# Blocks turned by VectorE and moved by way of DRAM instead of TensorE transposes, in a hybrid decoder layer

## The chip, the cores and the metric

The kernel runs on one core of a Trainium2 chip. The metric is the device time of one execution in microseconds, median of three runs. TensorE multiplies matrices, VectorE (DVE in the profile) and ScalarE (ACT) work on tiles, GpSimd (POOL) and SyncE (SP) issue DMAs. The profile is one more execution, taken by the hardware profiler.

## The reference

One decoder layer for 256 tokens and 2048 features, in float32. The input is normalised and projected; the projections feed two parallel mixers, whose outputs are merged under gates and projected once more.

```python
h = _rmsnorm(x, pre_norm_g)
proj = jnp.einsum('bsd,de->bse', h, w_in)
(q_a, c_kv, k_rope, z_mla, c_in, b_gate, c_gate, z_conv, g_mla, g_conv) = jnp.split(proj, cuts, axis=-1)
# latent attention, 16 heads: q from q_a, k_nope and v from c_kv, rotary parts, causal softmax p
attn = p @ v                                          # per head, 256 x 128
attn = attn.reshape(b, s, MLA_WIDTH) * jax.nn.silu(z_mla)
y_mla = jnp.einsum('bse,ed->bsd', attn, w_o_mla)
u = c_gate * c_in                                     # short convolution of 3 taps
conv = sum(conv_w[k] * u_pad[:, k:k + s] for k in range(CONV_K))
y_conv = jnp.einsum('bse,ed->bsd', b_gate * conv * jax.nn.silu(z_conv), w_o_conv)
merged = jax.nn.sigmoid(g_mla) * y_mla + jax.nn.sigmoid(g_conv) * y_conv
out = jnp.einsum('bsd,de->bse', merged, w_out)
x = x + _rmsnorm(out, post_norm_g)
```

## The kernel before

**Precision and weights.** Every float32 operand is split into a high and a low part (`split_act`: ScalarE writes the high part, VectorE subtracts for the low one), and a product is three matmuls: high by high, high by low, low by high. The weights come in units of 128 x 2048 elements in the order of the list `plan`. `take(i)` loads ahead into three raw buffers and splits one unit ahead, in halves of 1024 columns, into five pairs of buffers `whi` and `wlo`. SyncE issues the loads. TensorE's instructions, and operations marked by `keep_in_program_order`, keep the order of the program; the other operations of ScalarE and VectorE are placed by a scheduler when the program is built. On the chip each engine then runs its instructions in that fixed order.

**Stages.** First the two latents are projected and normalised (to about 60 us). Then a loop over 16 heads (60 to 600 us). A head `h` projects its gate (`project`, tile z), makes its scores and softmax (`scores`, tiles sc and p; p holds three 128 x 128 blocks: queries of the first tile by keys of the first, queries of the second by both), turns p so that keys lie on partitions (`turn`, tiles tp and pt) and multiplies by the values (`values`, tile o). In between the same head makes a quarter of the channels of the convolution branch: `channels(h, 0)` to `channels(h, 3)`, 24 products of weights with the normalised input each (tile cv, weights u_head). Four heads complete one block of 512 channels, in two token tiles, which `taps` moves along the tokens by DMA (tiles mv, cw, issued by POOL) and `channels_join` multiplies by the last factor. Every second head makes queries and keys for the next pair (`group_a`, tiles qn and kn), every fourth the values (`group_v`).

Then come four column blocks c (600 to 955 us). Each has four products over 2048 features, `tokens(c, n, ...)`: two gates from the input (n = 0, 1), the attention (n = 2), the channels (n = 3). `split_branch` splits the attention's outputs into at_both during the first, `turn_branch` turns the channel blocks into cv_both during n = 1 and 2 of c = 0. The merged block m of c is turned by `features` during the first product of c + 1, into m_both. Last the output product: four column blocks of four units each, the first one begun before the last merged block is turned.

All turning is done by TensorE: `transpose` into a PSUM bank, whose content is then split. `turn` makes three transposes of 128 x 128 a head, `turned` four for each of eight channel blocks and eight merged blocks. The product of probabilities and values begins with a matmul that reads both parts of pt:

```python
mm(both, vv[0][:, 0, vs], pt[:, :, :S], start=True, stop=False)
```

Many temporaries come from one pool, `bp`; when the heads are done it is closed, and at_both and cv_both lie in its memory.

Of the kernel before, what the change touches and what calls it, by code (L numbers as in the profile page):

```python
# [11 lines left out]
F32 = mybir.dt.float32  # L12
# [6 lines left out]
P = 128  # L19
S = 256  # L20
NT = S // P
D = 2048
KD = D // P
H = 16
# [58 lines left out]
def tile_layer(ctx: ExitStack, tc: tile.TileContext, xw, x, pos, pvec, post_g, wc, wz, wcv, wkr, wqk, wqr, wv, cwr, wsq, out):  # L83
    nc = tc.nc
# [15 lines left out]
    wpool = ctx.enter_context(tc.tile_pool(name="wpool", bufs=1))  # L100
    psum = ctx.enter_context(tc.tile_pool(name="psum", bufs=1, space=PSUM))


    plan = []

    def add(ap, width=UNIT):
        plan.append((ap, width))
        return len(plan) - 1
# [24 lines left out]
            u_head[i][j] = add(wcv[i, j - 1] if j else wz[i])  # L133

    u_d = [[[add(wsq[n, c, k]) for k in range(4)] for n in range(4)] for c in range(4)]
    u_out = [[add(wsq[4, c, k]) for k in range(4)] for c in range(4)]

    raws, splits, early = {}, {}, {}
    done = {"raw": 0, "split": 0}
# [13 lines left out]
    def split_unit(i):  # L153
        t, w = raws.pop(i), plan[i][1]
        parts = []
        if i == u_kr:
            t = t[:, :w].rearrange("p (k c) -> p k c", k=KD)
            for h in range(2):
                both = wpool.tile([P, HALF], F32R, name=f"whi{i}_{h}", tag="whi", bufs=5)
                both = both[:, :].rearrange("p (k j c) -> p k j c", k=KD // 2, j=2)  # L160
                ks = slice(h * KD // 2, (h + 1) * KD // 2)
                split_act(both[:, :, 0], both[:, :, 1], t[:, ks])
                parts.append(both.rearrange("p k j c -> p k (j c)"))
            splits[i] = parts
            return
        if i <= u_qa[-1]:

            hi, lo = (wpool.tile([P, HALF], F32R, name=f"{o}{i}", tag=o, bufs=5) for o in ("whi", "wlo"))
            for j in range(2):
                k, o = 2 * i + j, j * XW  # L170
                src = x_first if k == 0 else t[:, o : o + S]
                split_scaled(x_both, src, k)
                split_act(hi[:, j * R : (j + 1) * R], lo[:, j * R : (j + 1) * R], t[:, o + S : o + XW], True)
            splits[i] = [(hi, lo)]
            return
        for h in range(0, w, HALF):
            n = min(HALF, w - h)
            if u_out[3][0] <= i < u_out[3][3]:
                hi, lo = (op.tile([P, HALF], F32R, name=f"w{o}{i}_{h}") for o in ("hi", "lo"))
            else:  # L180
                hi = wpool.tile([P, HALF], F32R, name=f"whi{i}_{h}", tag="whi", bufs=5)
                lo = wpool.tile([P, HALF], F32R, name=f"wlo{i}_{h}", tag="wlo", bufs=5)
            split_act(hi[:, :n], lo[:, :n], t[:, h : h + n])
            parts.append((hi, lo))
        splits[i] = parts
# [23 lines left out]
    def bank(name, tag="mm", bufs=4):  # L209
        return psum.tile([P, 512], F32, name=name, tag=tag, bufs=bufs)  # L210
# [80 lines left out]
    def temp(name, shape=(P, S), dt=F32, bufs=2, tag=None):  # L291

        tag, n = tag or name.rstrip("0123456789_"), shape[-1]
        if n % LINE == 0:
            return bp.tile(list(shape), dt, name=name, tag=tag, bufs=bufs)
        return bp.tile([P, -(-n // LINE) * LINE], dt, name=name, tag=tag, bufs=bufs)[:, :n]


    def split_scaled(dst, src, k):
# [251 lines left out]
    def scores(h):  # L551
# [35 lines left out]
        for t in range(NT):  # L587
            o = slice(t * P, (2 * t + 1) * P)
            nc.vector.tensor_scalar(p[:, o], p[:, o], rs[:, t : t + 1], None, op0=ALU.mult)
        return p  # L590

    def turn(h, p):

        tp = bank(f"tp{h}", tag="st", bufs=1)
        for b in range(3):
            transpose(tp[:, b * P : (b + 1) * P], p[:, b * P : (b + 1) * P], ident[:, :])
        pt = temp("pt", (P, 2, 3 * P), F32R, 1)
        split_act(pt[:, 0, :], pt[:, 1, :], tp[:, : 3 * P])
        return pt

    def values(h, pt, sz):
# [52 lines left out]
    def channels_join(j, t):  # L654
        u, w = cv_t[:, j, t, :], cv_w[:, t, :]
        nc.vector.tensor_tensor(u, u, w, op=ALU.mult)

    def taps(j, t):

# [35 lines left out]
    for h in range(H):  # L695

        tapped = h % 4 == 2 or (h > 0 and h % 4 == 0) or h == H - 1
        sz_new = silu("sz", project(u_head[h][0], f"z{h}"))
        if h == 0:
            latent_turn("qa", qa, "q_g", (("st", 1), ("o", 1)))  # L700

            def turn_keys():
                latent_turn("ckv", ckv, "kv_g", (("mm", 4), ("mm", 4)))
                next(table_parts)

            channels(h, 0, turn_keys)
            for i in first:
                make(*i)
            key_rope()
            channels(h, 1)  # L710
            channels(h, 2)
            p = scores(h)
        elif h == 1:

            pt = turn(0, p)
            channels(h, 0)
            values(0, pt, sz)
            p = scores(h)
            channels(h, 1)
            channels(h, 2)  # L720
            pt = turn(h, p)
        else:
            p = scores(h)
            channels(h, 0)
            channels(h, 1)
            pt = turn(h, p)
            if tapped:
                next(tap)
            channels(h, 2)
            values(h, pt, sz_new)  # L730
            if tapped:
                next(tap)
        for i in made[h]:
            make(*i)
        if h == 1:
            values(h, pt, sz_new)
        sz = sz_new
        channels(h, 3)
        if h % 4 == 0 and h > 0:
            for t in range(NT):  # L740
                channels_join(h // 4 - 1, t)
        if h % 4 == 1:
            tap = taps(h // 4, 1)
            next(tap)
        elif h % 4 == 3 and h + 1 < H or h == H - 2:
            tap = taps(h // 4, 0)
            next(tap)
    for t in range(NT):
        channels_join(3, t)


    bstack.close()
# [8 lines left out]
            hs = slice(h, h + 2)  # L761
            split_act(at_both[:, hs, :S], at_both[:, hs, S:], at_f[:, hs, :], True)

    def turn_branch(i):

        j, t = divmod(i, NT)
        turned(f"ct{i}", cv_t[:, j, t, :], cv_both, j, t)

    def turned(name, src, both, c, t):
        tp = bank(name, tag=("st", "o")[t], bufs=1)  # L770
        for j in range(4):
            transpose(tp[:, j * P : (j + 1) * P], src[:, j * P : (j + 1) * P], ident[:, :])
        ks, ts = slice(4 * c, 4 * c + 4), slice(t * P, (t + 1) * P)
        lo = slice(t * P + S, (t + 1) * P + S)
        split_act(both[:, ks, ts], both[:, ks, lo], tp[:, :].rearrange("p (k q) -> p k q", k=4))

    def tokens(c, n, cols):

        pss = [bank(f"sq{c}_{n}_{t}") for t in range(NT)]
        for kk in range(4):  # L780
            w = take(u_d[c][n][kk])
            if c == 0 and n == 0:
                split_branch(kk)
            if c == 0 and n in (1, 2):
                turn_branch(4 * (n - 1) + kk)
            for t in range(NT):
                for k4 in range(4):
                    k = 4 * kk + k4
                    a = [cols[:, k, o + t * P : o + (t + 1) * P] for o in (0, S)]
                    product(pss[t][:, :], a, w(k4, 512), k == 0, k == KD - 1)  # L790
        return pss
# [4 lines left out]
    def features(c, m, m_both):  # L796

        for t in range(NT):
            turned(f"mt{c}_{t}", m[t], m_both, c, t)

    waiting = m_both = None
    for c in range(4):
# [18 lines left out]
        for t in range(NT):  # L821
            nc.vector.tensor_tensor(m[t][:, :], pss[t][:, :], m[t][:, :], op=ALU.mult)
        pss = tokens(c, 3, cv_both)
        for t in range(NT):
            y = gates[1][t]
            nc.vector.tensor_tensor(y[:, :], pss[t][:, :], y[:, :], op=ALU.mult)
            nc.vector.tensor_tensor(m[t][:, :], m[t][:, :], y[:, :], op=ALU.add)
        waiting = m
    def out_product(ps, t, w, kk):
        ts = slice(t * P, (t + 1) * P)  # L830
# [5 lines left out]
        for t in range(NT):  # L836
            out_product(pss[t], t, w, kk)

    pss = [bank(f"out0_{t}") for t in range(NT)]
    out_products(pss, take(u_out[0][0]), 0)  # L840
    features(3, waiting, m_both)
    main.close()


# [27 lines left out]
    def finish(t, rr):  # L872
        for a, b in ((0, 256), (256, 512), (512, 1024), (1024, 1536), (1536, 2048)):
# [3 lines left out]
            )  # L877
            nc.sync.dma_start(out=out[t * P : (t + 1) * P, cs], in_=og[:, t, cs])

    for c in range(3):  # L880
        if c:
            pss = [bank(f"out{c}_{t}") for t in range(NT)]
        for kk in range(0 if c else 1, 4):
            out_products(pss, take(u_out[c][kk]), kk)
        for t in range(NT):
            out_block(c, t, pss[t])
    nc.vector.reduce_sum(part[:, :], ssq[:, :, :3], axis=mybir.AxisListType.X)
    nc.vector.tensor_scalar(part[:, :], part[:, :], 1.0 / D, EPS, op0=ALU.mult, op1=ALU.add)
    pss = [bank(f"out3_{t}") for t in range(NT)]
    for t in range(NT):  # L890
        for kk in range(4):
            if t == 0:
                last.append(take(u_out[3][kk]))
            out_product(pss[t], t, last[kk], kk)
        finish(t, out_block(3, t, pss[t]))

# [89 lines left out]
```

## Time and profile before

| | |
|---|---|
| median of 3 runs | 1053.41 us (1053.41 to 1053.55) |
| the profiled execution | 1052.91 us, span 1050.9 us, granted TensorE clock 0.998 |
| DMA | 212.13 MB, mean 202 GB/s |
| heads, 100 to 350 us | TensorE busy 250.00, VectorE 181.59, ScalarE 151.10, POOL 14.43 us |
| column blocks, 665 to 960 us | TensorE busy 295.00, VectorE 150.02, ScalarE 123.65, POOL 0.00 us |

The span runs from the first to the last instruction; the execution's own time is some 2 us longer. The page gives the busy time of each engine, the chain of work that ended last (each step followed back to what released it), groups of instructions by source line, and DMA issues. Other views of the same trace list an engine's instructions in order of time (start, length, line, tile written <- tiles read, and in brackets its idle time before and what ended it), the waits by engine, and the time from a DMA's issue to its landing. PE is TensorE, PEld its weight loads. Line L88 is the helper `matmul`, L91 `transpose`, L228 and L229 the two halves of `split_act`, L664 the helper that issues the taps' DMAs.

### The profile page before, as it was taken

How to read it: one execution, taken by the hardware profiler on the slowest of the kernel's cores; microseconds unless marked ns; L12 is line 12 of the kernel's file. 1: busy time of each engine (PE TensorE's matmuls, PEld its weight loads, DVE VectorE, ACT ScalarE, POOL GpSimd, SP SyncE). 2: the span in 40 equal slices, each digit the busy share in tenths (PEclk: the TensorE clock that was granted, in tenths of full speed). 3: DMA queues.
4: the chain of work that ended last, by engine and by line, in shares of the span. 5: the costliest groups of instructions: out<-in, count | busy, mean ns of one | idle time of the engine just before them, and what ended most of it. 6: DMA issues, size and time to landing. Idle time of an engine off the chain costs nothing.

```text
span 1050.9 us, 12889 instructions
## 1 busy us (share of the span) xinstructions
PE 1041.9 (99%) x4934; PEld 874.3 (83%) x4934; DVE 670.0 (64%) x954; ACT 560.3 (53%) x770; POOL 71.4 (7%) x147
## 2 busy tenths in 40 slices
PE   9999999999999999999999999999999999999996
PEld 8888888888888888888888888888888888888885
DVE  7588668676686777866777764554554455445562
ACT  7776556556665566655655464444434434444450
POOL 7620011000110001100011000000000000000000
PEclk9999999999999999999999999999999999999999
DMA  8745566455665555845567555455555555558542
GB/s 332 298 173 200 201 219 207 165 210 200 210 215 196 189 192 175 273 172 193 188 203 236 202 184 196 166 195 200 190 187 184 200 200 190 176 195 314 196 171 80
DMA packets 33884, 212.13 MB, mean 202 GB/s; under 512 B 4320, under 2 KB 5024, under 8 KB 10912
## 3 DMA queue, kind: packets, MB, share of 16 engines
q1 hardware_dynamic: 29808, 197.54, 52.1%
q0 software_dynamic: 3584, 10.50, 4.2%
q10 hardware_dynamic: 432, 3.29, 0.8%
q8 instruction: 38, 0.62, 0.2%
q14 instruction: 22, 0.18, 0.0%
HBM read 205.05 MB, written 2.10 MB: 197 GB/s over the span
## 4 chain that ended last, share of the span: by engine, by line
PE 98%; issue 1%; DVE 0%; POOL 0%; ACT 0%; POOLq 0%; DVEq 0%; ACTq 0%
PE cv L88 33%; PE sq L88 33%; PE z L88 8%; PE out L88 7%; PE qn L88 2%; PE kn L88 2%; PE qa L88 2%; PE vv L88 2%; PE ckv L88 2%; PE sc L88 1%; PE qr L88 1%; PE o L88 1%; PE tp L91 0%; PE idle L88 0%; PE kr L88 0%
## 5 line engine op out<-in xcount | busy, mean ns | idle before, releaser
L229 DVE TENSOR_TENSOR wlo<-raw,whi 128x1024 fp32r<-128x1024 f32 (+1 forms) x370 | 440.3, 1199 | 309.4 <-ACT whi L228 285.5
L228 ACT ACTIVATE whi<-raw 128x1024 fp32r<-128x1024 f32 (+1 forms) x372 | 383.5, 1036 | 379.2 <-PE sq L88 186.3
L88 PE MATMUL cv<-whi,x_both 128*128 128x512 f32 x1024 | 325.4, 391 | 0.0
L88 PEld LDWEIGHTS cv<-whi,x_both 128*128 128x128 f32 x1024 | 192.3, 188 | 38.9
L88 PE MATMUL cv<-wlo,x_both 128*128 128x512 f32 x512 | 199.5, 390 | 0.0
L88 PE MATMUL sq<-whi,x_both 128*128 128x512 f32 x512 | 160.2, 391 | 0.0
L88 PEld LDWEIGHTS sq<-whi,x_both 128*128 128x128 f32 x512 | 96.1, 188 | 19.9
L88 PEld LDWEIGHTS cv<-wlo,x_both 128*128 128x128 f32 x512 | 96.2, 188 | 18.5
L88 PE MATMUL sq<-wlo,x_both 128*128 128x512 f32 x256 | 99.6, 389 | 0.0
L88 PE MATMUL sq<-whi,at_both 128*128 128x512 f32 x256 | 80.4, 391 | 0.0
L88 PE MATMUL sq<-whi,cv_both 128*128 128x512 f32 x256 | 79.5, 389 | 0.0
L88 PE MATMUL out<-whi,m_both 128*128 128x512 f32 x256 | 79.2, 390 | 0.0
L88 PE MATMUL z<-x_both,whi 128*128 128x512 f32 x256 | 60.7, 389 | 0.0
L88 PEld LDWEIGHTS sq<-whi,cv_both 128*128 128x128 f32 x256 | 48.0, 188 | 10.0
L88 PEld LDWEIGHTS sq<-whi,at_both 128*128 128x128 f32 x256 | 48.1, 188 | 9.9
L88 PEld LDWEIGHTS out<-whi,m_both 128*128 128x128 f32 x256 | 48.0, 188 | 9.9
L88 PEld LDWEIGHTS z<-x_both,whi 128*128 128x128 f32 x256 | 48.0, 188 | 9.9
L88 PEld LDWEIGHTS sq<-wlo,x_both 128*128 128x128 f32 x256 | 48.1, 188 | 9.8
L88 PE MATMUL sq<-wlo,at_both 128*128 128x512 f32 x128 | 49.8, 389 | 0.0
L88 PE MATMUL sq<-wlo,cv_both 128*128 128x512 f32 x128 | 49.8, 389 | 0.0
L88 PE MATMUL out<-wlo,m_both 128*128 128x512 f32 x128 | 49.8, 389 | 0.0
L88 PEld LDWEIGHTS z<-x_both,wlo 128*128 128x128 f32 x256 | 32.8, 191 | 1.2
(208 smaller groups left out, 1031.1 us busy)
## 6 DMA issues: line engine op xcount, KB each, us to landing
raw<-wsq_dram SPq DMA_DIRECT2D x80, 1024.0 KB, 4.7
raw<-wcv_dram SPq DMA_DIRECT2D x64, 1024.0 KB, 4.8
raw<-wz_dram SPq DMA_DIRECT2D x16, 1024.0 KB, 4.8
raw<-wqk_dram SPq DMA_DIRECT2D x8, 1024.0 KB, 6.0
cw<-cwr_dram POOLq DMA_DIRECT2D x24, 256.0 KB, 5.7
raw<-wc_dram SPq DMA_DIRECT2D x4, 1024.0 KB, 9.9
raw<-wv_dram SPq DMA_DIRECT2D x4, 1024.0 KB, 6.7
cv_f<-x_dram SPq DMA_DIRECT2D x1, 2048.0 KB, 9.5
```

Source lines behind the costliest of these rows:

```text
L88: return tc.keep_in_program_order(nc.tensor.matmul(*a, **kw))
L228: a = nc.scalar.activation(hi, src, AF.Copy)
L229: b = nc.vector.tensor_tensor(lo, src, hi.bitcast(F32), op=ALU.subtract)
```

## The change

VectorE's transpose instruction turns blocks of 32 x 32 within a tile. `turned` lets VectorE turn all of them at once into a second tile (`via`), four DMAs then write it to DRAM (`go`), so that the blocks change their place between groups of 32 partitions, and a fifth reads the whole back over the source (`come`). All five are issued by POOL. The returned block is split from SBUF.

- Heads 2 to 15: `scores` turns p and issues the four writes; `come` follows after `channels(h, 1)`, and for heads that carry taps also after the first step of the taps. `turn` then only splits: in odd heads after `channels(h, 2)`, in even ones after `channels(h, 3)`. `values` of an even head is made in the next head after its `channels(h, 0)`; that of an odd head after its `group_a`, that of head 15 at the end. Heads 0 and 1 turn p on TensorE as before.
- Channels: `channels_join` turns each block as soon as it is complete, for tile 1 one head earlier than before; `split_channels` takes the place of `turn_branch`.
- Merged blocks: turned at the end of each c, with the gate's tile as `via`; `features` only splits.
- Output: units of blocks 0 and 1 are loaded and multiplied in the order of `out_order`; the first three quarters of both come before the fourth, which is the one that needs the last merged block. The split of that block is written in the program ahead of the third unit.

```diff
-    u_out = [[add(wsq[4, c, k]) for k in range(4)] for c in range(4)]
+    out_order = [(c, k) for c in range(2) for k in range(3)] + [(0, 3), (1, 3)]
+    out_order += [(c, k) for c in (2, 3) for k in range(4)]
+    u_out = {ck: add(wsq[4, ck[0], ck[1]]) for ck in out_order}
...
+    def turned(src, via, n):
+        via = via[:, : P * n]
+        v = via.rearrange("p (q k x) -> p q k x", q=4, k=n)
+        nc.vector.transpose(v.rearrange("p q k x -> p k q x"), src)
+        far = dram.tile([P, P * n], F32, name="far", tag=f"far{n}", bufs=2)
+        def go():
+            f = far[:, :].rearrange("(q y) (i m) -> i y q m", q=4, i=4)
+            for i in range(4):
+                m = via[32 * i : 32 * i + 32, :].rearrange("y (q m) -> y q m", q=4)
+                tc.keep_in_program_order(nc.gpsimd.dma_start(out=f[i], in_=m))
+        def come(dst):
+            tc.keep_in_program_order(nc.gpsimd.dma_start(out=dst, in_=far[:, :]))
+        return go, come
+    def turned_back(src, via, n):
+        go, come = turned(src, via, n)
+        go()
+        come(src)
...
+    def via():
+        return temp("via", (P, 512), bufs=1)
...
-        return p
+        if h < 2:
+            return p, None
+        go, come = turned(p[:, :], via(), 3)
+        go()
+        return p, come
     def turn(h, p):
-        tp = bank(f"tp{h}", tag="st", bufs=1)
-        for b in range(3):
-            transpose(tp[:, b * P : (b + 1) * P], p[:, b * P : (b + 1) * P], ident[:, :])
         pt = temp("pt", (P, 2, 3 * P), F32R, 1)
-        split_act(pt[:, 0, :], pt[:, 1, :], tp[:, : 3 * P])
+        if h < 2:
...
+            return pt
+        hi, lo = (pt[:, j : j + 1, :].rearrange("p o (k q) -> p (o k) q", k=3) for j in range(2))
+        split_act(quarters(hi), quarters(lo), by_rows(p[:, :], 3), True)
         return pt
...
         nc.vector.tensor_tensor(u, u, w, op=ALU.mult)
+        turned_back(u, via() if t or j < 3 else temp("mv2", (P, 512), bufs=1, tag="mv2x"), 4)
...
         else:
-            p = scores(h)
+            p, come = scores(h)
             channels(h, 0)
+            if h % 2 and h > 2:
+                values(h - 1, pt, sz)
             channels(h, 1)
-            pt = turn(h, p)
             if tapped:
                 next(tap)
+            come(p[:, :])
             channels(h, 2)
-            values(h, pt, sz_new)
             if tapped:
                 next(tap)
+            if h % 2:
+                pt = turn(h, p)
         for i in made[h]:
             make(*i)
-        if h == 1:
-            values(h, pt, sz_new)
+            if i[0] == "a":
+                values(h, pt, sz_new)
         sz = sz_new
         channels(h, 3)
+        if h > 0 and h % 2 == 0:
+            pt = turn(h, p)
+        if h == H - 1:
+            values(h, pt, sz)
         if h % 4 == 0 and h > 0:
-            for t in range(NT):
-                channels_join(h // 4 - 1, t)
+            channels_join(h // 4 - 1, 0)
+        if h % 4 == 3:
+            channels_join(h // 4, 1)
...
-    def turned(name, src, both, c, t):
-        tp = bank(name, tag=("st", "o")[t], bufs=1)
-        for j in range(4):
-            transpose(tp[:, j * P : (j + 1) * P], src[:, j * P : (j + 1) * P], ident[:, :])
+    def split_turned(src, both, c, t):
         ks, ts = slice(4 * c, 4 * c + 4), slice(t * P, (t + 1) * P)
         lo = slice(t * P + S, (t + 1) * P + S)
-        split_act(both[:, ks, ts], both[:, ks, lo], tp[:, :].rearrange("p (k q) -> p k q", k=4))
+        split_act(quarters(both[:, ks, ts]), quarters(both[:, ks, lo]), by_rows(src, 4), True)
...
+        steps = []
         for t in range(NT):
             y = gates[1][t]
             nc.vector.tensor_tensor(y[:, :], pss[t][:, :], y[:, :], op=ALU.mult)
             nc.vector.tensor_tensor(m[t][:, :], m[t][:, :], y[:, :], op=ALU.add)
+            steps.append(turned(m[t][:, :], y[:, :], 4))
+        for go, _ in steps:
+            go()
+        for t, (_, come) in enumerate(steps):
+            come(m[t][:, :])
...
-    pss = [bank(f"out0_{t}") for t in range(NT)]
-    out_products(pss, take(u_out[0][0]), 0)
-    features(3, waiting, m_both)
+    pss = [[bank(f"out{c}_{t}") for t in range(NT)] for c in range(2)]
+    for i, (c, kk) in enumerate(out_order[:3]):
+        w = take(u_out[c, kk])
+        if i == 2:
+            features(3, waiting, m_both)
+        out_products(pss[c], w, kk)
```

More of the change, by code (lines that the diff above doesn't have):

```diff
@@ L101, in tile_layer @@
     psum = ctx.enter_context(tc.tile_pool(name="psum", bufs=1, space=PSUM))
+    dram = ctx.enter_context(tc.tile_pool(name="dram", bufs=1, space=bass.MemoryType.DRAM))
     plan = []
@@ L177, in split_unit @@
             n = min(HALF, w - h)
-            if u_out[3][0] <= i < u_out[3][3]:
+            if u_out[3, 0] <= i < u_out[3, 3]:
                 hi, lo = (op.tile([P, HALF], F32R, name=f"w{o}{i}_{h}") for o in ("hi", "lo"))
@@ L296, in temp, with by_rows, quarters @@
         return bp.tile([P, -(-n // LINE) * LINE], dt, name=name, tag=tag, bufs=bufs)[:, :n]
+    def turned(src, via, n):
[15 more added lines that the diff above has]
+        come(src)
+    def by_rows(t, n):
+        return t.rearrange("p (i k x) -> p k i x", i=4, k=n)
+    def quarters(t):
+        return t.rearrange("p k (i x) -> p k i x", i=4)
+    def via():
+        return temp("via", (P, 512), bufs=1)
     def split_scaled(dst, src, k):
@@ L589, in scores @@
             nc.vector.tensor_scalar(p[:, o], p[:, o], rs[:, t : t + 1], None, op0=ALU.mult)
-        return p
+        if h < 2:
[3 more added lines that the diff above has]
+        return p, come
     def turn(h, p):
-        tp = bank(f"tp{h}", tag="st", bufs=1)
-        for b in range(3):
-            transpose(tp[:, b * P : (b + 1) * P], p[:, b * P : (b + 1) * P], ident[:, :])
         pt = temp("pt", (P, 2, 3 * P), F32R, 1)
-        split_act(pt[:, 0, :], pt[:, 1, :], tp[:, : 3 * P])
+        if h < 2:
+            tp = bank(f"tp{h}", tag="st", bufs=1)
+            for b in range(3):
+                transpose(tp[:, b * P : (b + 1) * P], p[:, b * P : (b + 1) * P], ident[:, :])
+            split_act(pt[:, 0, :], pt[:, 1, :], tp[:, : 3 * P])
+            return pt
+        hi, lo = (pt[:, j : j + 1, :].rearrange("p o (k q) -> p (o k) q", k=3) for j in range(2))
+        split_act(quarters(hi), quarters(lo), by_rows(p[:, :], 3), True)
         return pt
@@ L711, in tile_layer @@
             channels(h, 2)
-            p = scores(h)
+            p, _ = scores(h)
         elif h == 1:
@@ L717, in tile_layer @@
             values(0, pt, sz)
-            p = scores(h)
+            p, _ = scores(h)
             channels(h, 1)
@@ L722, in tile_layer @@
         else:
-            p = scores(h)
+            p, come = scores(h)
             channels(h, 0)
+            if h % 2 and h > 2:
+                values(h - 1, pt, sz)
             channels(h, 1)
-            pt = turn(h, p)
             if tapped:
                 next(tap)
+            come(p[:, :])
             channels(h, 2)
-            values(h, pt, sz_new)
             if tapped:
                 next(tap)
+            if h % 2:
+                pt = turn(h, p)
         for i in made[h]:
             make(*i)
-        if h == 1:
-            values(h, pt, sz_new)
+            if i[0] == "a":
+                values(h, pt, sz_new)
         sz = sz_new
         channels(h, 3)
+        if h > 0 and h % 2 == 0:
+            pt = turn(h, p)
+        if h == H - 1:
+            values(h, pt, sz)
         if h % 4 == 0 and h > 0:
-            for t in range(NT):
-                channels_join(h // 4 - 1, t)
+            channels_join(h // 4 - 1, 0)
+        if h % 4 == 3:
+            channels_join(h // 4, 1)
         if h % 4 == 1:
@@ L747, in tile_layer @@
             next(tap)
-    for t in range(NT):
-        channels_join(3, t)
+    channels_join(3, 0)
     bstack.close()
@@ L762, in split_branch, with split_channels @@
             split_act(at_both[:, hs, :S], at_both[:, hs, S:], at_f[:, hs, :], True)
-    def turn_branch(i):
-        j, t = divmod(i, NT)
-        turned(f"ct{i}", cv_t[:, j, t, :], cv_both, j, t)
-    def turned(name, src, both, c, t):
-        tp = bank(name, tag=("st", "o")[t], bufs=1)
-        for j in range(4):
-            transpose(tp[:, j * P : (j + 1) * P], src[:, j * P : (j + 1) * P], ident[:, :])
+    def split_turned(src, both, c, t):
         ks, ts = slice(4 * c, 4 * c + 4), slice(t * P, (t + 1) * P)
         lo = slice(t * P + S, (t + 1) * P + S)
-        split_act(both[:, ks, ts], both[:, ks, lo], tp[:, :].rearrange("p (k q) -> p k q", k=4))
+        split_act(quarters(both[:, ks, ts]), quarters(both[:, ks, lo]), by_rows(src, 4), True)
+    def split_channels(i):
+        j, t = divmod(i, NT)
+        split_turned(cv_t[:, j, t, :], cv_both, j, t)
     def tokens(c, n, cols):
@@ L784, in tokens @@
             if c == 0 and n in (1, 2):
-                turn_branch(4 * (n - 1) + kk)
+                split_channels(4 * (n - 1) + kk)
             for t in range(NT):
@@ L798, in features @@
         for t in range(NT):
-            turned(f"mt{c}_{t}", m[t], m_both, c, t)
+            split_turned(m[t][:, :], m_both, c, t)
     waiting = m_both = None
@@ L878, in finish @@
             nc.sync.dma_start(out=out[t * P : (t + 1) * P, cs], in_=og[:, t, cs])
+    for c, kk in out_order[3:6]:
+        out_products(pss[c], take(u_out[c, kk]), kk)
     for c in range(3):
[L881 to L884, printed above, removed]
+        if c == 2:
+            pss.append([bank(f"out{c}_{t}") for t in range(NT)])
+        for kk in range(4) if c == 2 else (3,):
+            out_products(pss[c], take(u_out[c, kk]), kk)
         for t in range(NT):
-            out_block(c, t, pss[t])
+            out_block(c, t, pss[c][t])
     nc.vector.reduce_sum(part[:, :], ssq[:, :, :3], axis=mybir.AxisListType.X)
@@ L892, in tile_layer @@
             if t == 0:
-                last.append(take(u_out[3][kk]))
+                last.append(take(u_out[3, kk]))
             out_product(pss[t], t, last[kk], kk)
```

## The prediction

> **What bounds the kernel now.** I read the page first (busy shares, chain), then what TensorE waited for, then the chain in order of time.
>
> ```profile
> PE 1041.9 (99%) x4934; PEld 874.3 (83%) x4934; DVE 670.0 (64%) x954; ACT 560.3 (53%) x770; POOL 71.4 (7%) x147
> ...
> PE 98%; issue 1%; DVE 0%; POOL 0%; ACT 0%; POOLq 0%; DVEq 0%; ACTq 0%
> ```
>
> TensorE is busy from end to end and 98% of the chain is its own. The view of waits for TensorE holds one line, at the start:
>
> ```profile
> PE idle L88 <- POOL hpi L252: 1.1, 1, 1.1
> ```
>
> So each matmul taken from TensorE's stream shortens the run, and each new wait of TensorE lengthens it. The chain in order of time shows what a transpose takes of that stream, and what stands where in head 5:
>
> ```profile
> 251.85 0.33 PE tp L91 x3
> ...
> 258.23 2.80 PE qn L88 x16
> 261.03 2.79 PE kn L88 x16
> 263.82 5.47 PE cv L88 x24
> ...
> 622.10 0.44 PE ct L91 x4
> ...
> 713.01 0.87 PE mt L91 x8
> ```
>
> Pieces follow without a gap, so 0.33 us for three is what would be saved, though one transpose's row says 271 ns.
>
> **What is removed.** 42 transposes of heads 2 to 15 (14 x 0.33 = 4.62 us), 32 of the channels (8 x 0.44 = 3.52) and 32 of the merged blocks (4 x 0.87 = 3.48): 106 in all, 11.6 us. No matmul is added; the reordering of values and of the output units moves matmuls without changing their number.
>
> **What is added beside the path.** VectorE gets 14 block transposes of 128x384 and 16 of 128x512. No row shows this instruction. The nearest are the 128x384 split into pt at 0.55 us and 128x512 operations at 0.69; below lies the 128x256 scale of p at 0.35, above four passes over 32 rows (1.71 us for the four rp_b). I take 0.55 and 0.69: 18.7 us for an engine that is busy 180 of 250 us in the head stage and waits for ScalarE and TensorE in between. Dearer ones first delay blocks, priced below.
> POOL issues 30 x 5 = 150 DMAs. Rows:
>
> ```profile
> L664 POOL DMA_DIRECT2D mv<-cv_f x24: 502/542/612, 131.6 to 571.1; - x24
> L664 POOL DMA_DIRECT2D cw<-cwr_dram x24: 546/556/578, 136.6 to 592.2; - x24
> DMA to landing us min/median/max: 4.3/4.3/4.3
> ```
>
> At 0.55 us that is 82 us on POOL (7% busy). The third row is the landing of a cw loaded alone, at 154 us; the eight lone ones took 3.4 to 5.2. The mv copies, three issued back to back, mostly landed in 2.6 to 3.2, at most 5.6. So I put the last of a block's four writes at 3.0 us (2.6 to 5.6; a write to DRAM of this kind has no row) and the read back at 4.3 (3.4 to 5.2). From the end of the VectorE transpose a block is back after 3 x 0.55 to the last issue, 3.0, 4.3 and 0.1 for semaphores: 9.0 us (7.7 to 12.5). POOL waits in it for the writes to land; behind it stand only the taps' copies and the next block's writes, none of them wanted in those 3 us. The 13.8 MB of traffic is 6.5% more; weights land in 4.7 us and are loaded two units (10.9 us) ahead of their split.
>
> **Where a returning block meets the queues.** ScalarE and VectorE run in order; both now wait at the split of a returned block, and the weight splits behind it wait too. The changed program as built fixes the order on each engine. I place each split by what stands ahead of it (a weight half waits until the fifth one before it is used up) and by durations of before; times count from the end of the head's scores.
> - Heads 3, 7, 11: p is scaled 5.3 us after the scores (215.64 less 210.34 in head 4), turned at 5.9, back at 15 (13.6 to 18.4). The split follows a weight half freed by the end of channels(h,2): 3 x 5.45 + 0.57 for values(h-1) = 16.9, and 1.06 for that half, 18. values(h) comes after qn and kn, 16.9 + 2.80 + 2.79 = 22.5. Nothing is paid.
> - Even heads: the read back is queued on POOL behind the third cw, which waits for VectorE's tap products (about 18); the block is back at about 24, its split stands at 26, values(h) in the next head at 35. Nothing.
> - Head 15: back at 15 to 17, wanted at 22. Nothing.
> - Merged blocks, from the end of the tokens: turned at 4.2, back at 13 (12 to 17). Their split stands at 16, and TensorE has weights until 27. The last one has the six output units ahead of it, 33 us. Nothing.
> - End of the heads: the first at_both split waits until the temporaries' pool is free, now also for the last block's writes: turned 4.6 us after the last channels, two sets of writes at 1.65 + 3.0 with one issue between, 14.4. The split stands at 18; TensorE would starve from about 21. Nothing, but thin.
> - Heads 5, 9, 13: here the order itself costs. ScalarE's exponentials now stand behind half<-o of the head before, and the pt split stands behind the evacuation of kn:
>
> ```
> ScalarE  ... half<-kn3_0, qn_hi, half<-kn3_1, pt<-p (waits for the DMA), kn, kn, half<-o5
> VectorE  ... wlo54_0, qn_lo, qn_lo, pt<-p,pt (waits for the DMA), f<-kn, f<-kn
> TensorE  ... qn3, kn3, o5<-pt,vv
> ```
>
> TensorE wants both halves of pt the moment kn ends. The same stretch of before, ScalarE and then VectorE in the timeline:
>
> ```profile
> 262.90 1.06 ACT L228 ACTIVATE whi<-raw 128x1024 fp32r<-128x1024 f32 x1 [1.18 <-PE kn L88]
> 263.87 0.40 ACT L228 ACTIVATE qn_hi<-f 128x256 fp32r<-128x256 f32 x1
> 264.17 0.37 ACT L350 ACTIVATE half<-kn 128x256 f32<-128x256 f32 x1
> 264.44 0.41 ACT L228 ACTIVATE qn_hi<-f 128x256 fp32r<-128x256 f32 x1
> 264.74 0.38 ACT L350 ACTIVATE half<-kn 128x256 f32<-128x256 f32 x1
> ```
>
> ```profile
> 263.99 1.23 DVE L229 TENSOR_TENSOR wlo<-raw,whi 128x1024 fp32r<-128x1024 f32 x1 [0.89 <-ACT whi L228]
> 265.14 0.76 DVE L229 TENSOR_TENSOR qn_lo<-f,qn_hi 128x256 fp32r<-128x256 f32 x2
> 265.81 0.75 DVE L351 TENSOR_TENSOR f<-kn,half 128x256 f32<-128x256 f32 x2
> ```
>
> kn ends at 263.82. The hi split can run from 265.05 (0.47), the lo split from 265.81 (0.55), and o5 starts at 266.4: TensorE stands 2.58 us, three times: 7.7 us. Below this the floor is 0.37 + 0.47 + 0.55 = 1.4 each on idle engines; nothing behind the splits can give time back, since TensorE sets the end.
> It also needs p back by 263.82 + 1.2, which is 23.7 us after head 5's scores. The chain there: a weight half freed at 4.1 ends at 5.2; table load and sz to 6.8, another half to 7.9, half<-o4 to 8.2, table load to 9.5, exponentials to 10.7; reciprocal, at_f, scale and turn to 12.5; trip 9.0: back at 21.5 (20.2 to 25.0). It just fits.
>
> **The sum.** 11.6 - 7.7 = 3.8 us. The profiled execution has a span of 1050.9 and took 1052.91; I expect 1047.1 and 1049.1. The median of before lies 0.5 above that execution: 1053.41 - 3.8 = 1049.6. With stalls of 1.4 to 3.9 us (the latest return within the bounds) this case covers 1046.0 to 1053.5.
>
> **Rivals.**
> 1. *No stall*: the three splits run before kn ends and all 11.6 us stay: 1041.9. Against it, engines run in order and the timeline's order of before matches its built order line by line. 0.08.
> 2. *The trip is long (slower).* From a trip of 9.0 + 2.2 us on, each further us costs 1 us in each of heads 5, 9, 13; beyond 12.5 the change loses. [...] If each of the five issues waits out one 1.22 us weight subtraction, the trip is 15.1, p is 3.9 us late, and the time 1049.6 + 11.7 = 1061.3; waits of half that length (trip 12.05) give 1052.2. Against: 48 POOL issues of before took 502 to 612 ns beside a VectorE that was busy 72% of that stage. 0.13.
> [...]
> 3. *The clock falls after a stall (slower).* TensorE never paused here, and the granted clock is 0.998. If the channels block after a pause ran at half speed for half its 5.47 us, each stall would cost 2.7 more: 1049.6 + 8.2 = 1057.8. In the only pause of before, its end, the granted clock still reads 1.00 in the two slices of 2 us after the last matmul. 0.06.
> [...]
> 4. *The end of the heads stalls.* If at_both also waits for the last read back (20 or later), TensorE stands up to 4 us once: 1053.6. 0.07.
>
> **How the numbers follow.** The main case has 0.66. A measurement of this kernel tells about 0.2% (2.1 us) from no change. Faster: main case but for its upper edge (0.64) and rival 1 (0.08), 0.72. Same: that edge, rival 4 and the milder half of rival 2: 0.14. Slower: the rest, 0.14. The range 1045.0 to 1055.5 leaves out rival 1 and the far ends of 2 and 3, about 0.18.
>
> **What would show it.** Right: in the changed profile TensorE waits for VectorE's pt split three times, 2.6 us each, in heads 5, 9, 13; transposes gone but for 22; nothing else over 0.5 us. Wrong: no such wait (rival 1); the wait 4 us or longer with ScalarE's pt waiting for a DMA (2); matmuls longer than 391 ns after a pause (3); a wait near 600 us (4).

## The result, and the profile after

The change made the kernel slower: 1060.42 us median (1058.12 to 1063.63) against 1053.41 before, a ratio of 1.007 with a 95% interval of 1.0047 to 1.0094. The forecast was 1049.6, faster. The profiled execution took 1060.42 us with a span of 1058.5, so it is itself the median.

The page, busy shares and chain:

```profile
PE 1034.1 (98%) x4828; PEld 867.6 (82%) x4828; DVE 685.0 (65%) x984; ACT 560.4 (53%) x770; POOL 155.1 (15%) x297
...
PE 91%; DMA 4%; issue 2%; DVE 2%; POOL 1%; ACT 0%; POOLq 0%; DVEq 0%; ACTq 0%
```

TensorE has 106 matmuls fewer and 7.8 us less busy time, but its share of the chain fell from 98% to 91%: DMAs, VectorE and GpSimd now stand on the path. The view of waits for TensorE names one new wait:

```profile
PE o L88 <- DVE pt L234: 13.6, 3, 7.2
```

Three waits, 13.6 us, all for VectorE's split of pt ahead of the values. The chain in order of time shows the second one, in head 9 (start, duration, what):

```profile
395.11 2.78 PE qn L88 x16
397.93 0.23 ACT half L389
398.19 0.39 ACT half L389
398.57 0.46 issue
399.03 4.07 DMA p<-far
403.12 0.53 ACT pt L233
403.68 0.57 DVE pt L234
404.25 0.14 issue
404.38 1.41 PE o L88 x4
405.79 6.46 PE cv L88 x24
```

The read back of p is on the path, then both halves of the split, then the values. The last two lines hold what the sum had at nothing: four matmuls that took 0.57 us before take 1.41, and a block of 24 that took 5.47 takes 6.46. The view by windows, around the first pause (head 5: TensorE idle from 261.33 to 264.02), shows the granted clock in its column PEclk, the third from the right:

```profile
262.50:264.00 1.50, 0.00 (x0) 0.01 (x1) 1.50 (x5) 0.54 (x2) 0.00 (x0) 1.00 1.02 431
264.00:265.00 1.00, 0.98 (x5) 0.96 (x6) 0.84 (x3) 0.75 (x2) 0.00 (x0) 0.72 0.03 8
265.00:266.00 1.00, 1.00 (x4) 0.81 (x3) 0.87 (x3) 0.38 (x1) 0.00 (x0) 0.50 0.00 0
266.00:267.00 1.00, 1.00 (x3) 0.72 (x3) 0.43 (x2) 0.00 (x0) 0.00 (x0) 0.50 0.00 0
267.00:268.00 1.00, 1.00 (x4) 0.80 (x3) 0.00 (x0) 0.00 (x0) 0.00 (x0) 0.57 0.00 0
```

The granted clock drops to 0.50 when TensorE is already at work again (at 264.44 by the trace's clock records), and stays there 3.41 us.

Where the 7.6 us of span went, by the starts of stages in both traces: from the scores of head 0 to those of head 15 13.5 more (487.2 to 500.7); from there to the token products 0.2 more; the token products 6.5 less (354.7 to 348.2); the output product 0.9 less; the stretch from VectorE's last operation to the end 1.8 more (3.4 to 5.2); the start 0.5 less, which varies by 0.8 between the kernels here. Inside the heads, from the scores of head 5 to those of head 6 took 39.54 us, of 9 to 10 40.56, of 13 to 14 43.89; a kernel without the pauses (below) takes 35.03 each time. So the three heads lose 18.9 us: 13.6 of waiting and 5.3 of slow clock behind it.

### The profile page after: what moved, and what is told of

The parts are those of the page before. It is cut to its first block, busy times and chain, and to the rows that moved or that the text cites. A ratio compares the mean times of both kernels' runs of the same rounds, so it can differ in the third digit from the quotient of the medians.

```text
span 1058.5 us, 13010 instructions
## 1 busy us (share of the span) xinstructions
PE 1034.1 (98%) x4828; PEld 867.6 (82%) x4828; DVE 685.0 (65%) x984; ACT 560.4 (53%) x770; POOL 155.1 (15%) x297
## 4 chain that ended last, share of the span: by engine, by line
PE 91%; DMA 4%; issue 2%; DVE 2%; POOL 1%; ACT 0%; POOLq 0%; DVEq 0%; ACTq 0%
PE sq L88 33%; PE cv L88 30%; PE z L88 7%; PE out L88 7%; PE vv L88 2%; PE qa L88 2%; PE ckv L88 2%; PE qn L88 2%; DMA far<-via 2%; PE kn L88 2%; PE sc L88 1%; DMA cw<-cwr_dram 1%; PE o L88 1%; PE qr L88 1%; DMA p<-far 1%
## 5 line engine op out<-in xcount | busy, mean ns | idle before, releaser
L315 POOL DMA_DIRECT2D far<-via x84 | 46.1, 555 | 243.0 <-DVE via L308 240.3
L315 POOL DMA_DIRECT2D far<-sg x32 | 17.4, 551 | 315.1 <-DVE sg L308 241.9
```

The source lines that it names most:

```text
L315: tc.keep_in_program_order(nc.gpsimd.dma_start(out=f[i], in_=m))
```

## The experiments

Theory A: the three pauses and the slow clock behind them are the whole loss of the head stage, and they come from where pt's split stands in the queues. Rival B: the transfers themselves, by GpSimd's queue or by their traffic, cost the time wherever the split stands.

**The block given a cover.** Heads 5, 9 and 13 treated as the even heads are:

```
+    def late(h):
+        return 1 < h < H - 1 and h % 4 != 3
...
-            if h % 2 and h > 2:                  # values(h - 1) behind channels(h, 0)
+            if h > 2 and late(h - 1):
...
-            if h % 2:                            # turn(h, p) ahead of made
+            if not late(h):
...
-            if i[0] == "a":                      # values(h) behind qn, kn
+            if i[0] == "a" and not late(h):
...
-        if h > 0 and h % 2 == 0:                 # turn(h, p) behind channels(h, 3)
+        if late(h):
```

> Heads 5, 9 and 13 split their returned block after their last channel unit and make its values in the next head, as the even heads do; all else is as in the change. Theory A (the three pauses of TensorE, 13.6 us, and the slow clock behind each, 5.2 us in all, are the whole loss of the head stage): no wait of TensorE for pt, granted clock 0.998, the profiled span falls by 18.8 from 1058.5 to about 1039.7, time about 1041.6. Rival B (the transfers themselves slow the stage, by held queues or weight loads that come later; the pauses only move): a wait of several us stands elsewhere in heads 5, 9 or 13, time 1048 or more. Rival C (a late block holds ScalarE's weight splits instead): 1043 to 1046, with waits of TensorE for whi or wlo.

1042.29 us, ratio 0.9896 (0.9882 to 0.9911), granted clock 0.998, and no wait for pt is left. It lies 0.7 above theory A's figure and below the range of C (the late block holding ScalarE's weight splits); B falls. The transfers land no earlier (p's writes 4.9 us median against 4.7), so what the run gets back comes from the cover alone.

**Only the blocks.** Heads turned on TensorE as before, the two other kinds of block through DRAM:

> The heads are as before the change (their 42 transposes on TensorE, values in the same head); channel and merged blocks go through DRAM and the output order is the new one. Theory A: only the stages behind the heads gain, 6.5 + 0.9 us by the stage times of the change, so 1053.4 - 7.4 = 1046.0 and no wait of TensorE. Rival B (the blocks' transfers cost the head stage something by themselves, at the joins of heads 4, 8, 12): 1048 to 1053.

1045.78 us, ratio 0.9931 (0.9914 to 0.9947), no wait of TensorE over 0.2 us: theory A's 1046.0. This half of the change does what the sum said.

**Only the heads.** Channel and merged blocks turned on TensorE as before:

> Only the heads' blocks go through DRAM; channel and merged blocks are turned on TensorE as before. On ScalarE the pt split of heads 5, 9 and 13 now stands ahead of the qn evacuation, as in heads 3, 7 and 11, not behind kn's. Theory A (what cost the pauses was the exponentials behind the head before and the channel block's transfer ahead of p's on POOL): no wait for pt over 1 us, 1053.4 - 4.6 = 1048.8. Rival B (a trip of 11 us is too long in these heads whatever stands ahead): pauses of 1 to 4 us in 5, 9, 13 with 1.7 us of slow clock each, 1055 to 1062.

1052.41 us, ratio 0.9993 (0.9984 to 1.0002), between the two. TensorE never waits for pt, and from the scores of head 0 to those of head 15 it takes 481.8 us, 5.4 less than before: theory A holds in the heads, where this build, too, puts the split ahead of qn's evacuation. But the gain is lost again at the end. From VectorE's last operation to the end of the span pass 8.0 us here, 3.4 before. The trace's instruction records show GpSimd in a closing DRAIN instruction, which the views leave out, until 1049.88 while SyncE was through at 1045.4; that drain took 10.65 us, against 4.93 before, where SyncE was the later of the two. Neither theory had this in it.

**Another queue.** All transfers stay, issued by SyncE:

```
-  tc.keep_in_program_order(nc.gpsimd.dma_start(out=f[i], in_=m))
+  tc.keep_in_program_order(nc.sync.dma_start(out=f[i], in_=m))
...
-  tc.keep_in_program_order(nc.gpsimd.dma_start(out=dst, in_=far[:, :]))
+  tc.keep_in_program_order(nc.sync.dma_start(out=dst, in_=far[:, :]))
```

> As the change, but all writes and reads of the blocks are issued by SyncE's queue, between the weight loads, not by GpSimd. If GpSimd's queue makes the landing slow (4.7 us median for p's writes): writes land in about 2.4 us, the trip falls from 11.2 to about 8. If the weight loads in flight do it: p's writes that meet a 1 MB load still land in 4 to 6 us, and the read back behind such a load in 5 or more. The order of the splits changes too (pt ahead of qn's evacuation in heads 5, 9, 13), so pauses for pt should go: 1042 to 1046, unless SyncE's wait for the writes delays weight loads by more than the 10.9 us of cover; then TensorE waits for whi and the time is above 1050.

1040.14 us, ratio 0.9875 (0.986 to 0.989), the fastest of all kernels here, 13.0 us below before. No wait of TensorE but the start's; 35.03 us from the scores of head 5 to those of head 6. The DMA lists, p's writes, first of the change and then of this kernel (KB each, us from issue to landing):

```profile
far<-via POOLq DMA_DIRECT2D x56, 48.0 KB, 4.7
```

```profile
far<-via SPq DMA_DIRECT2D x56, 48.0 KB, 1.7
```

The same 48 KB land 3.0 us sooner. An issue takes SyncE about 0.43 us, GpSimd 0.55. The order that the build fixes changed as well, in two places. ScalarE in head 9:

```profile
378.73 0.40 ACT L621 ACTIVATE p<-p,nb 128x128 f32<-128x128 f32 x1
...
381.52 0.36 ACT L389 ACTIVATE half<-o 128x256 f32<-128x256 f32 x1
...
388.67 0.53 ACT L233 ACTIVATE pt<-p 128x384 fp32r<-128x384 f32 x1 [2.22 <-DMA p<-far]
...
393.56 0.64 ACT L389 ACTIVATE half<-qn 128x256 f32<-128x256 f32 x2
```

In heads 5, 9 and 13 pt's split now stands ahead of qn's evacuation instead of behind kn's. The exponentials also stand ahead of half<-o instead of behind it, so the transpose of p ends 6.9 to 7.3 us after the scores, where it ended 12.1 to 14.2 after them in the change. So the trip, the place of the split and the time of the transpose all changed, and the next runs part the first two.

**The order alone.** The SyncE kernel, with the split asked for later in heads 5, 9, 13:

```
-            if h % 2:
+            if h % 2 and (h % 4 == 3 or h == 1):
                 pt = turn(h, p)
             ...
             if i[0] == "a":
+                if h % 4 == 1 and h > 1:
+                    pt = turn(h, p)
                 values(h, pt, sz_new)
```

> The kernel with all transfers on SyncE's queue (1040.1 us, no pause, trip about 8 us), with one edit: in heads 5, 9, 13 the split of pt is asked for behind qn and kn, so that it stands behind kn's evacuation on ScalarE and VectorE as it did in the change, one or two operations later still. If the order alone makes a pause however early the block is back: three pauses of 2.6 to 3.6 us for VectorE's pt, each with 1.7 us of slow clock, 1040.1 + 13 to 16 = 1053 to 1056. If the trip made them: no pause over 1 us and 1040 to 1042.

1061.08 us, ratio 1.0072 (1.0057 to 1.0087): 20.9 us lost by this edit alone, more than expected. The transposes are as early as without it (6.9 to 7.2 us after the scores). Its waits:

```profile
PE o L88 <- DVE pt L234: 13.0, 3, 4.3
```

In head 5 the read back was issued at 249.65, and this kernel's read backs landed in 5.1 us, so the block lay ready from about 255; its split began at 265.10, behind kn's, and TensorE waited 4.34 us. All three pauses are 4.34. From their heads' scores to the next ones' take 40.99, 42.19 and 41.22 us, 19.3 more than 3 x 35.03: 13.0 of waiting and 6.3 behind it. In this order the pauses come although the block is back some 10 us before its split begins.

**The slow trip alone.** Only the channel blocks on SyncE, p on GpSimd:

```
-    def turned(src, via, n):
+    def turned(src, via, n, q=nc.gpsimd):
...
-                tc.keep_in_program_order(nc.gpsimd.dma_start(out=f[i], in_=m))
+                tc.keep_in_program_order(q.dma_start(out=f[i], in_=m))
...
-            tc.keep_in_program_order(nc.gpsimd.dma_start(out=dst, in_=far[:, :]))
+            tc.keep_in_program_order(q.dma_start(out=dst, in_=far[:, :]))
...
     def turned_back(src, via, n):
-        go, come = turned(src, via, n)
+        go, come = turned(src, via, n, nc.sync)
```

> The change with only the channel and merged blocks' transfers on SyncE's queue; p's stay on GpSimd, and GpSimd issues 122 DMAs in all. In heads 5, 9, 13 pt stands ahead of qn's evacuation. If the pauses came from the order: none here, though p's writes still land in 4 to 5 us. If p's slow trip made them: pauses of 1 to 4 us, 1050 or more. The end: GpSimd's closing drain took 10.65 us in the kernel with 122 GpSimd DMAs, 7.88 with 202, 4.93 with 52 and 2.08 with 132. If the number of GpSimd DMAs sets it, it is 10.65 again, the run ends 8.0 us after the last product with gamma, and the time is 1040.1 + 4.5 = 1044.6; if not, 1040 to 1042.

The expectation has two errors: the merged blocks stayed on GpSimd, and it issues 162 DMAs, not 122. 1040.88 us, ratio 0.9884 (0.9869 to 0.9898). p's writes still land in 4.2 us, the split stands ahead of qn's evacuation, and the only wait for pt is 0.2 us. With a split in that place GpSimd's slower trip cost TensorE no more than that 0.2 us. Here, too, p was turned early, 6.8 to 8.5 us after the scores; what this place of the split would cost with p turned as late as in the change no run shows. The closing drain took 4.53 us and was hidden.

**Only the writes on SyncE.** The first pair of lines of the queue experiment without the second:

> The change with all writes of the blocks on SyncE's queue and the reads back on GpSimd (82 DMAs of GpSimd in all). If GpSimd as issuer makes the writes land late: 1.7 us here against 4.7, and the trip of p about 8 us. If it is the weight loads in flight: 4 us or more. pt stands ahead of qn's evacuation, so no pause: 1040 to 1043; the closing drain lies between 4.9 and 10.7 us, at 7.9 by the nearest count (74 of 128 left over).

1041.42 us, ratio 0.989 (0.9874 to 0.9907). p's writes land in 1.7 us with the same weight loads in flight, where the run above, with p turned about as early, had 4.2: for p's writes the difference goes with the issuing engine, not with the traffic. The closing drain took 7.38 us and ended 1.2 us after SyncE; against the all-SyncE kernel this one is 1.3 longer.

**A scale for pauses.** Twelve pauses of TensorE behind the heads of the covered kernel:

```
+    def pause(n):
...
+        matmul(ps[:, :P], ones[:, :], ones[:, :], start=True, stop=True)
+        tc.keep_in_program_order(nc.vector.tensor_copy(tiny[:, :], ps[:, :LINE]))
+        for i in range(n):
+            tc.keep_in_program_order(nc.gpsimd.memset(tiny[:, :], 1.0))
+        matmul(ps[:, :LINE], ones[:, :], tiny[:, :], start=True, stop=True)
...
+            if c and kk == 1:
+                pause(PAUSES[4 * (c - 1) + n])
```

> The covered kernel (1042.3 us) with twelve pauses of TensorE put into the token products behind the heads, each the round trip of a small matmul to VectorE, 0 to 40 short GpSimd memsets and back, so of lengths from under 1 us to some 6 us. Theory: the granted clock goes to 0.5 some 3.1 us after a pause begins, even if TensorE is at work again by then, if the pause was longer than a limit between 0.5 and 2.7 us, and stays there 3.3 us, so a pause beyond the limit costs about 1.7 us on top of its length and a shorter one nothing. [...] The total is 1042 plus the pauses, 20 to 40 us, plus 1.7 for each that trips the clock.

One run of 1114.33 us. Two pauses and what followed, from TensorE's timeline and the windows:

```profile
761.51 0.41 PE L89 MATMUL pz<-tiny,ones 128*128 128x32 f32 x2 [2.02 <-POOL tiny L841]
...
816.70 0.41 PE L89 MATMUL pz<-tiny,ones 128*128 128x32 f32 x2 [2.75 <-POOL tiny L841]
```

```profile
763.50:764.50 1.00, 1.00 (x6) 0.84 (x5) 0.00 (x0) 0.00 (x0) 0.00 (x0) 1.00 0.82 344
...
818.70:820.70 2.00, 2.00 (x6) 1.58 (x5) 0.00 (x0) 0.00 (x0) 0.00 (x0) 0.50 0.03 12
```

Pauses of 0.93, 1.31, 1.66 and 2.02 us left the clock at 1.00: the next 40 matmuls took 9.2 us. After 2.75, 3.11 and 3.48 us the clock was 0.50 and they took 10.8, so 1.6 us each on top; after 4.56 to 8.20 us 11.0 to 11.9. So the limit that the theory put between 0.5 and 2.7 us lies, in these pauses, between 2.02 and 2.75. The trace's clock records say more: every slow stretch of this run but the one that its end cuts short is 3.41, 6.83 or 10.24 us long, one, two or three times 3.413, and they begin at multiples of 3.413 from each other. The change's own trace has the same: slow stretches of 3.413, 3.413 and 6.827 us that begin at 264.44, 404.38 and 544.33, each 41 times 3.413 after the one ahead. So the records can be laid on windows of 3.413 us at whose ends the clock changed. Laying the pauses of five traces on those windows (the change twice, the late split, the filled pauses and this run; 23 pauses), each pause with 2.00 us or more of idle time in one window was followed by the drop at that window's end; none with at most 1.94 was.

**Pauses filled, and the change again.** The change with idle work in TensorE's pauses, and the change itself beside it:

```
+  keep_busy(h, {5: 12, 9: 16, 13: 31}.get(h, 0))   # matmuls of 128x512 nobody reads (body left out)
   values(h, pt, sz_new)
```

> The change with 12, 16 and 31 idle matmuls of 128x512 (0.228 us each: 2.7, 3.6 and 7.1 us) put ahead of the values of heads 5, 9 and 13, whose results nothing reads, so that TensorE works while it would wait; the order on the other engines stays as in the change. If the slow clock behind the pauses is a price of its own (18.8 us lost in the three heads, of which 13.6 are waiting): no granted clock of 0.5 before the end, and the run is 5.2 us shorter than the change, about 1055, though TensorE runs 59 matmuls more. [...]

> The change itself, unaltered, on the same chip beside the kernel with filled pauses: 1058 to 1064 as in its five runs, three pauses for pt of 2.7, 3 to 4.5 and 5 to 8 us, each with a granted clock of 0.5 behind it for 3.4 us or twice that. If the place of the 3.4 us windows differs from run to run, a pause near 2 to 2.7 us may be without it.

The filled kernel took 1057.97 us (1055.58 to 1060.53), the change beside it 1063.83 (1058.42 to 1067.89): 5.9 less, near the 5.2 expected, though both spread too far to call that a measurement of it. With the pauses filled the profile has no clock of 0.5 before the end, and cv matmuls at 0.39 to 0.40 us. TensorE still paused twice, for 1.18 and 3.03 us; the longer pause fell 1.94 and 1.09 on two windows. In its head 13 the block came later than in the profile of the change, and that profiled run gained nothing in span.

The change again is the better witness. Its profile has pauses of 2.69 us in heads 5 and 9 alike; windows across what follows each:

```profile
264.70:268.00 3.30, 3.23 (x12) 2.64 (x13) 2.11 (x6) 1.07 (x3) 0.00 (x0) 0.70 0.03 10
268.00:271.00 3.00, 3.00 (x12) 2.43 (x11) 0.75 (x1) 0.00 (x0) 0.00 (x0) 0.76 0.00 0
...
404.10:407.00 2.90, 2.88 (x14) 2.48 (x15) 2.06 (x6) 1.07 (x3) 0.00 (x0) 1.00 0.05 20
407.00:411.00 4.00, 4.00 (x19) 3.30 (x19) 1.59 (x2) 1.63 (x2) 0.52 (x1) 1.00 0.01 1
```

The first has the slow clock (0.70 and 0.76, the means of its two stretches), the second not (1.00). One window held 2.16 us of the first pause; the second fell 1.14 and 1.56 on two. From the scores of head 5 to those of head 6 took 39.55 us, of 9 to 10 37.95: 1.6 us for where the window's edge happened to be. That the spread of the change's time (9.5 us here, against 0.4 of the covered kernel) comes from this edge and from late blocks is likely, but not shown.

## Why the prediction was wrong, step by step

- *What is removed*: right in kind, a little small. Without pauses and with a hidden drain the change gains 13.0 us (the SyncE kernel) where the sum had 11.6: about 0.12 us for a transpose instead of 0.11.
- *What is added beside the path*: right. VectorE's block transposes:

```profile
L308 DVE STREAM_TRANSPOSE via<-p 128x384 f32<-128x384 f32 x14 | 8.1, 579 | 3.0 <-DMA far<-via 2.5
L308 DVE STREAM_TRANSPOSE sg<-sg 128x512 f32<-128x512 f32 x8 | 5.7, 712 | 0.3
```

  0.58 and 0.71 us, for 0.55 and 0.69. The last column holds something that I had not seen coming: p's transposes waited 2.5 us for writes out of `via`.
- *Where a returning block meets the queues*: right for the other heads, head 15, the merged blocks and the end of the heads; TensorE waits nowhere else. Right too for the price of the order: 2.58 us worked out, 2.69 measured in head 5, and in head 9 of the second profile of the change.
- *The trip, and the way to it*: too small. In head 9 the trip ran from the end of the transpose at 391.88 to the block's return at 403.1, 11.2 us, inside my bounds; in head 13, from 532.69 to 546.97, 14.3, outside them. The term that failed most is the landing of the last write, 3.0 by the mv copies: it took 4.6 in heads 5 and 9 and 6.5 in head 13 (the median of all p's writes is 4.7). The way to the transpose failed as well: it ended 13.7 and 14.2 us after the scores in heads 9 and 13, where I had 12.5. The views of ScalarE in head 9 and of VectorE in head 13 say why:

```profile
386.03 0.42 ACT L666 ACTIVATE sz<-sl_f 128x256 f32<-128x256 f32 x1 [1.31 <-DVE sl_f L393]
```

```profile
532.11 0.58 DVE L308 STREAM_TRANSPOSE via<-p 128x384 f32<-128x384 f32 x1 [2.11 <-DMA far<-via]
```

  In head 9 sz, ahead of the exponentials, waited for VectorE. In head 13 p was scaled by 530.00, but `via`, of which there is one, still held the channel block ahead, which its writes to DRAM had yet to read out; GpSimd had stood 2.66 us between the first and second of them, in each profile of the change and of its covered and filled kernels, always between its 121st and 122nd DMA. Why it stood is open, and so is what a second `via` would give. Together the block was back 24.9 and 28.4 us after the scores of heads 9 and 13, for the 21.5 that I had and the 23.7 that I allowed. So "it just fits" failed, and the stall of head 9 grew to 3.72, of head 13 to 7.23: 5.9 us more than 3 x 2.58.
- *A pause costs its length*: the mistake in the mechanism. I gave the clock a rival of 0.06 and reasoned from the end of the run before, where the clock still read 1.00 up to 3 us after the last matmul (1043.04). The next slice of the same view has the fall:

```profile
1046.00:1048.00 2.00, 0.00 (x0) 0.00 (x0) 1.56 (x3) 0.00 (x0) 0.00 (x0) 0.76 0.82 303
```

  By the clock records it came at 1047.03, 4.0 us after that matmul, and went to 0.50; so the trace of before did show that a long pause costs the clock, though not how short a one does. Every pause of the change's profile was followed by it, the one of 2.69 us in head 5 too: 5.3 us. In the traces laid on windows of 3.413 us, 2.00 us of idle time within one was enough.
- *The end*: not in the sum. GpSimd's closing drain took 7.88 us against 4.93, ended 1.8 us after SyncE, and held the run for that long.

Put together: 1049.6 - 1.4 + 5.9 + 5.3 + 1.8 = 1061.2; measured 1060.42.

Of the rivals none was the case by itself. The second had the late block right but not where the time goes: issues took 0.55 us as before, where it supposed 1.22 more for each, and it was the landing that was late. The third's fall of the clock came in all three heads, to the 0.50 that it supposed, at 1.6 to 1.8 us each for its 2.7. p's writes landed in 4.7 us from GpSimd's queue and in 1.7 from SyncE's; what makes the 3.0 us no run here shows. The merged blocks' writes landed in 2.4 from GpSimd's queue (2.0 and 3.1 from SyncE, in the kernels with all and with only the writes there), in a stage where VectorE was busy 52% of the time, against 74% in the heads.

## What to carry to other kernels

Where one engine sets the end, price a wait of it not by its length alone but with what its clock does afterwards: here a pause of 2.7 to 3.7 us cost 1.6 to 1.8 us more, save two (2.69 and 3.03 us) that fell on two windows, with at most 1.94 us in either. When a block takes a detour through DRAM, look less at the trip's mean than at where its consumer stands in the in-order queues: with the split ahead of qn's evacuation the slow trip cost 0.2 us of waiting in all, and with the split behind kn's even a block 10 us early cost over 4 us a head. Then try the same transfers on another issuing queue: two words of code gave back 20 us here, by way of the order that the build then fixed, for with the order put back the same queue lost 20.9.

## What the hardware showed that I had not expected

- By the records above the clock fell and rose at the ends of windows of 3.413 us, and where those ends lay against the program changed from run to run: the drop came 3.1 us after the start of head 5's pause in one profile of the change and 3.9 in the other. Of equal pauses of 2.69 us two were followed by 0.50, with 2.69 and 2.16 us in one window, and one was not, with 1.14 and 1.56 in two. Over the 23 pauses the dividing line lies between 1.94 and 2.00 us of idle time in one window, by the modelled ends of the matmuls.
- Where GpSimd's closing drain ended after SyncE, the run ended with it. Its length differed with the number of DMAs that GpSimd issued, but did not simply grow with it: 4.93 us with 52, 7.38 with 82, 10.65 with 122, 2.08 with 132, 4.53 with 162, 7.88 with 202. Between 2.08, 4.93, 7.88 and 10.65, and between 4.53 and 7.38, the steps are 2.77 to 2.95 us, close to the 2.66 us for which GpSimd stood in head 13. That the two are one thing is a guess. One expectation above counts the DMAs beyond a multiple of 128; that was an estimate of mine, no run shows such a step, and the 7.9 us that it gave for 82 DMAs came out at 7.38. Where the drain ended after SyncE's last wait it lengthened the run: by 1.8 us in the change and its covered kernel, 1.2 with only the writes on SyncE, 4.5 in the heads-only kernel.
